# Input projection of a hybrid diffusion backbone: the order of its tiles, three convolution tiles between those of the queries

## Chip, cores and metric

The kernel runs on one core of one Trainium2 chip. Times are device microseconds of that core. TensorE (PE) multiplies matrices, PEld is its loading of weights, VectorE (DVE) and ScalarE (ACT) work elementwise, GpSimd (POOL) and SyncE (SP) issue DMAs, and POOL does a few small copies.

## What is computed

Two layers over 512 latent tokens (x) and 256 context tokens (ctx), model width 1024, float32. One input projection feeds three groups of heads; their outputs are joined and projected, and a SwiGLU feed-forward follows. The context takes part in the second layer only through its keys, values and GLA state.

```python
def layer(x, ctx, mod_x, mod_c, ..., ctx_out):
    hx = rmsnorm(x, g1) * (1 + sc1) + sh1
    hc = rmsnorm(ctx, g1) * (1 + csc1) + csh1
    (xc_in, xc_b, xc_c, xq, xk, xv, xgq, xgk, xgv, xgg, xlr) = jnp.split(hx @ w_in, COL_SPLITS, axis=-1)
    ...
    conv_x = short_conv(xc_in, xc_b, xc_c, conv_w)
    attn_x = window_attention(apply_rope(xq), apply_rope(xk), xv, k_ctx, v_ctx, sink)
    gla_x, gla_c = gla_bidir(xgq, xgk, xgv, xlr, xgg, ...)
    x = x + gt1 * (jnp.concatenate([conv_x, attn_x, gla_x], axis=-1) @ w_out)
    x = x + gt2 * swiglu(rmsnorm(x, g2) * (1 + sc2) + sh2, w_up, w_down)
    ...
```

## The kernel before, in words

Activations lie transposed, 128 features by up to 768 tokens. Every float32 operand of a dense product is split into a high and a low part, and a product is made of three: high by high, high by low, low by high. A **dense tile** (`dense_pass`, L754) makes 128 output columns: eight blocks of the contraction by three products, 24 matmuls of 512 columns for the latent tokens, and 24 of 256 for the context. Its weights come through a ring of four `raw` buffers; ScalarE casts the high part (`whi`) and VectorE subtracts for the low part (`wlo`, two buffers each), in `w_advance` (L541).

`IN_ORDER` (L427) lists the tiles of the input projection: `lr`, `gk`, `gq`, `gv`, `gg` of the GLA (its gates' input, keys, queries, values and output gate, two head pairs 0 and 1), `k`, `v`, `q0` to `q3` of the attention, and `cc`, `cx`, `cb` of the convolution (its two factors and its gate, two halves). The plan of weight loads (L463) and the loop that computes the tiles (L1888) both follow it. In the first layer one tile of modulation weights follows each of them, from the fifth on. In the second layer `q`, the convolution, `gq` and `gg` are made for the latent tokens alone.

Three things happen to a finished tile. `ev` (L1763) takes it out of its `main` bank of PSUM: a `q`, `v` or `cc` tile by a ScalarE copy, a `gk` tile by ScalarE and VectorE, `cx` by a VectorE product with `cc`, `cb` by five VectorE operations (three taps, product with the tile, split). `after` (L1836) prepares it: a `q` tile is rotated (four VectorE operations) and split (two more), `gq` starts a **GLA chain** (`gla_task`, L1284), and a `q` tile starts six attention blocks (four in the second layer; `attn_task`, L1481).

These chains are generators. A planner (`Plan`) keeps an estimated clock for each engine and, after each contraction block of a dense tile, lets those chains go a step whose inputs it thinks ready and whose buffers fit (`poll`, L294; `until`, L305). One GLA chain may be under way at a time, and three attention blocks. Behind the first tiles of a layer the exact order on each engine is no longer pinned (`S.strict = False`, L1901), and the framework's scheduler may still move single instructions.

A GLA chain forms gate values (matmuls with `gw`), then passes through seven levels. Each level is a group of 64x64 matmuls (a **gram**), a VectorE merge of its result (`COPY_PREDICATED`), two or three VectorE products on 128x768 elements that prepare the next level, and a ScalarE copy. An attention block is scores, maximum and sum on VectorE, exponentials on ScalarE, transposes, copies, value products, and a split into the tile `ca` that the second part of the output projection reads.

Behind the input projection stand the part of the output projection that reads convolution and GLA (`o1`, eight tiles), a wait for all attention blocks (L1922), and the part that reads attention (`o2`, L1952).

Temporary tiles come from a pool `t3` of 14 buffers, others from `act` of 20, PSUM from 3 `main` and 5 `bank` (L39). `cc`'s buffer is held until `cb` of the same half has been taken out.

Of the kernel before, what the change touches and what calls it, by code (L numbers as in the profile page):

```python
# [319 lines left out]
def hybrid_kernel(ctx: ExitStack, tc: tile.TileContext, x, c, cx, c_ctx, w_mod, b_mod, norm1_g, norm2_g,  # L320
# [97 lines left out]
    def out2_item(l, m, hold):  # L418
        def load(raw):
# [4 lines left out]
        w_item((l, "o2", m), 4, load, P, hold)  # L424

    N_OUT2, N_DOWN = 1, 3
    IN_ORDER = ("lr", "gk0", "gq0", "gv0", "k", "v", "q0", "gk1", "gq1", "gv1", "q1", "q2", "q3",  # L427
                "cc0", "cx0", "cb0", "cc1", "cx1", "cb1", "gg0", "gg1")
    IN_COL = dict(lr=W_LR, k=W_K, v=W_V)
    for i in range(2):  # L430
        IN_COL.update({f"gk{i}": W_GK + i * P, f"gq{i}": W_GQ + i * P, f"gv{i}": W_GV + i * P,
# [4 lines left out]
    def first_item(l, q):  # L436

        def load(raw):
            ks = slice(q * 2 * P, (q + 1) * 2 * P)
            r = []  # L440
            for i, name in enumerate(FIRST):
                for j in range(3 if name == "lr" else 1):
                    n, c0 = (32, IN_COL[name]) if name == "lr" else (P, IN_COL[name])
                    r.append((raw[:, :, i * P + j * n:i * P + (j + 1) * n],
                              w_in[l, ks, c0:c0 + n].rearrange("(k p) n -> p k n", p=P)))
            return r
        w_item((l, "first", q), 2, load, 4 * P)
        plan[-1]["quad"] = True
        plan[-1]["late"] = q > 0 or l == 0
        plan[-1]["apart"] = q + l == 0  # L450
# [9 lines left out]
    for l in range(DEPTH):  # L460
        for q in range(4 if l else 0):
            first_item(l, q)
        for i, name in enumerate(IN_ORDER):  # L463
            if name in FIRST:
# [1266 lines left out]
    for l in range(DEPTH):  # L1731
# [155 lines left out]
        X = None  # L1887
        for j, name in enumerate(IN_ORDER):  # L1888
            if name in FIRST:
# [194 lines left out]
```

## Time and profile before

| | |
|---|---|
| median of 3 runs | 1619.19 us (1618.64 to 1624.01) |
| the profiled execution | 1613.43 us, its span 1611.6 us |
| granted TensorE clock, mean | 0.997 |
| instructions | 29142 |
| DMA | 184.39 MB, 114 GB/s over the span |

The span runs from the first instruction to the last. In the first layer the tiles of the input projection behind the first four begin at 70 us and `o2` begins at about 391 us; in the second they begin at 988 us and `o2` at about 1216 us. A window's row gives the busy time of each engine in that stretch, and what is missing to its length is idle. An engine executes its own instructions in order, so an instruction that waits holds up those behind it.

### The profile page before, as it was taken

The page shows a single profiled execution, that of the slowest core. Times are in us where ns is not written, and L with a number is a line of the kernel's source. Part 1 is how long each engine was busy: PE and PEld are TensorE (multiplying, and loading weights), DVE is VectorE, ACT ScalarE, POOL GpSimd, SP SyncE. Part 2 cuts the span into 40 slices and gives each one's busy share as a digit, 9 for nine tenths or more (in the row PEclk, how much of TensorE's full clock was granted, in tenths as well). Part 3 has the DMA queues.
Part 4 walks back from the last instruction along what each step waited for, and adds up shares of the span by engine and source line. Part 5 has one row for each costly group of instructions (what it writes and reads, how often), then busy time and mean ns, then how long its engine had stood idle before and what let it go on. Part 6 is the DMA issues. An engine that isn't in the chain of part 4 may idle for free.

```text
span 1611.6 us, 29142 instructions
## 1 busy us (share of the span) xinstructions
PE 1569.9 (97%) x11530; PEld 1387.9 (86%) x11530; DVE 1219.3 (76%) x2426; ACT 757.0 (47%) x1596; POOL 105.2 (7%) x122
## 2 busy tenths in 40 slices
PE   7999999999999999999999999998999999999998
PEld 5778777888888899999999988786889989989898
DVE  5687886668886788788888877879787956747576
ACT  4455544453663243242433546464474744536354
POOL 2000000000000000000000010000001112213012
PEclk9999999999999999999999999999999999999999
DMA  9831222253224544435334342211225466858552
GB/s 256 247 113 28 82 64 71 62 170 109 75 79 146 156 132 144 143 118 156 93 108 127 91 133 66 53 40 41 66 85 120 94 148 139 173 126 160 147 123 93
DMA packets 277578, 184.39 MB, mean 114 GB/s; under 512 B 30853, under 2 KB 258753, under 8 KB 277441
## 3 DMA queue, kind: packets, MB, share of 16 engines
q1 hardware_dynamic: 251008, 155.93, 33.7%
q0 software_dynamic: 24608, 21.27, 7.7%
q10 hardware_dynamic: 1824, 5.31, 0.9%
q8 instruction: 91, 1.49, 0.4%
q14 instruction: 47, 0.38, 0.1%
HBM read 175.14 MB, written 7.34 MB: 113 GB/s over the span
## 4 chain that ended last, share of the span: by engine, by line
PE 75%; DVE 10%; DMA 3%; ACT 3%; issue 2%; DVEq 0%; SPq 0%; ACTq 0%
PE main L139 49%; PE bank L139 24%; DVE act L188 3%; PE bank L143 3%; DMA raw<-in_w_mod_dram 2%; DVE t L188 1%; DVE wlo L188 1%; DMA raw<-in_w_up_dram 1%; ACT t L155 1%; DVE t L216 1%; DVE t L199 1%; DVE mx L207 1%; ACT t L177 1%; DVE t L193 0%; ACT whi L177 0%
## 5 line engine op out<-in xcount | busy, mean ns | idle before, releaser
L139 PE MATMUL main<-act,whi 128*128 128x512 f32 (+2 forms) x2772 | 667.8, 345 | 5.6 <-DVE act L199 2.1
L139 PEld LDWEIGHTS main<-act,whi 128*128 128x128 f32 x2772 | 460.5, 189 | 63.6 <-issue 12.1
L139 PE MATMUL main<-act,wlo 128*128 128x512 f32 (+2 forms) x1866 | 477.7, 334 | 3.0 <-DVE wlo L188 3.0
L139 PEld LDWEIGHTS main<-act,wlo 128*128 128x128 f32 x1866 | 315.1, 189 | 31.7 <-DVE wlo L188 5.2
L177 ACT CAST whi<-raw 128x512 fp32r<-128x512 f32 (+4 forms) x242 | 181.5, 751 | 292.6 <-PE main L139 201.0
L139 PE MATMUL bank<-act,whi 128*128 128x256 f32 (+2 forms) x1140 | 208.9, 309 | 1.1 <-DVE whi L188 0.7
L139 PEld LDWEIGHTS bank<-act,whi 128*128 128x128 f32 x1140 | 178.5, 190 | 8.1 <-DVE whi L188 1.0
L139 PE MATMUL bank<-act,wlo 128*128 128x256 f32 (+2 forms) x898 | 171.7, 308 | 2.2 <-DVE wlo L188 2.2
L199 DVE SCALAR_TENSOR_TENSOR act<-main,mods,act 128x256 f32<-128x256 f32 (+1 forms) x162 | 99.1, 615 | 78.1 <-PE main L139 76.6
L139 PEld LDWEIGHTS bank<-act,wlo 128*128 128x128 f32 x898 | 142.8, 190 | 6.3 <-DVE wlo L188 3.2
L188 DVE TENSOR_TENSOR wlo<-raw,whi 128x1024 fp32r<-128x1024 f32 (+4 forms) x122 | 122.6, 1005 | 20.7 <-ACT whi L177 19.9
L188 DVE TENSOR_TENSOR wlo<-raw,wlo 128x512 fp32r<-128x512 f32 x120 | 81.6, 686 | 39.4 <-ACT wlo L177 38.7
L199 DVE SCALAR_TENSOR_TENSOR t<-raw,cst,t 128x512 f32<-128x512 f32 x126 | 92.1, 745 | 20.4 <-DMA raw<-in_w_mod_dram 19.8
L188 DVE TENSOR_TENSOR whi<-raw,whi 128x512 fp32r<-128x512 f32 x120 | 81.3, 686 | 26.2 <-ACT whi L177 24.6
L155 ACT ACTIVATE t<-bank,nm 128x256 f32<-128x256 f32 (+1 forms) x144 | 69.8, 497 | 60.4 <-DVE nm L199 55.7
L177 ACT CAST wlo<-raw 128x512 fp32r<-128x512 f32 x120 | 74.6, 622 | 40.9 <-PE main L139 17.4
L177 ACT COPY t<-bank 128x512 f32<-128x512 f32 (+3 forms) x131 | 57.4, 453 | 72.1 <-PE bank L139 43.5
L139 PE MATMUL main<-act 128*128 128x256 f32 (+1 forms) x516 | 79.5, 309 | 0.0
L188 DVE TENSOR_TENSOR act<-t,act 128x512 fp32r<-128x512 f32 (+7 forms) x110 | 73.1, 681 | 7.0 <-ACT act L177 5.2
L155 ACT ACTIVATE t<-t 128x256 f32<-128x256 f32 (+3 forms) x108 | 58.1, 538 | 41.8 <-DVE t L188 41.3
L139 PE MATMUL main<-t,whi 128*128 128x512 f32 (+1 forms) x302 | 75.9, 338 | 0.0
L139 PEld LDWEIGHTS main<-act 128*128 128x128 f32 x516 | 70.9, 191 | 5.2 <-ACT t L155 0.4
(162 smaller groups left out, 2007.3 us busy)
## 6 DMA issues: line engine op xcount, KB each, us to landing
raw<-in_w_mod_dram SPq DMA_DIRECT2D x92, 512.0 KB, 4.3
raw<-in_w_up_dram SPq DMA_DIRECT2D x80, 512.0 KB, 4.6
raw<-in_w_in_dram SPq DMA_DIRECT2D x26, 512.0 KB, 3.9
t<-in_w_up_dram POOLq DMA_DIRECT2D x40, 256.0 KB, 5.2
raw<-in_w_down_dram SPq DMA_DIRECT2D x24, 384.0 KB, 3.9
raw<-in_w_down_dram SPq DMA_DIRECT2D x32, 256.0 KB, 2.8
raw<-in_w_down_dram SPq DMA_DIRECT2D x16, 320.0 KB, 3.4
raw<-in_w_up_dram POOLq DMA_DIRECT2D x20, 256.0 KB, 4.7
```

The costliest lines, as they stand in the source:

```text
L139: self.pin("pe", self.nc.tensor.matmul(out, lhsT, rhs, start=start, stop=stop, **kw))
L143: self.pin("pe", self.nc.tensor.transpose(out, in_, ident))
L155: ins = self.pin("act", self.nc.scalar.activation(out, in_, func, **kw))
L177: self.pin("act", self.nc.scalar.copy(out, in_))
L188: self.pin(eng, self._v(eng).tensor_tensor(out, a, b, op))
L199: self.pin(eng, self._v(eng).scalar_tensor_tensor(out, a, s, b, op0, op1))
L207: self.pin("dve", self.nc.vector.tensor_reduce(out, in_, AX.X, op))
L216: self.pin("dve", self.nc.vector.copy_predicated(out, mask, data))
```

## The change

`IN_ORDER` is another list. `cc0` moves to the place behind `q0`, `cx0` to the place behind `q1`, `cb0` and `cc1` behind `q2`; `cx1`, `cb1` follow `q3`, and `gg0`, `gg1` stay last. Everything else is the same text, and the number of instructions of each kind on each engine is the same.

```diff
-    IN_ORDER = ("lr", "gk0", "gq0", "gv0", "k", "v", "q0", "gk1", "gq1", "gv1", "q1", "q2", "q3",
-                "cc0", "cx0", "cb0", "cc1", "cx1", "cb1", "gg0", "gg1")
+    IN_ORDER = ("lr", "gk0", "gq0", "gv0", "k", "v", "q0", "cc0", "gk1", "gq1", "gv1", "q1", "cx0", "q2", "cb0",
+                "cc1", "q3", "cx1", "cb1", "gg0", "gg1")
```

The first place is TensorE's order in the first layer, second GLA chain, ahead of its last gram (the last row of each piece; only its first matmul is shown). `main_2631` is the tile `cc0`, `t3_1816` and `t3_1817` the probabilities of an attention block that are being transposed. Before:

```order
L143 MATMUL bank_2538<-tab_82,t3_1816 128x128 x4
L143 MATMUL bank_2539<-tab_82,t3_1817 128x128 x4
L139 MATMUL main_2631<-act_496,wlo_2393 128x512
L139 MATMUL main_2631<-act_559,whi_2392 128x512 x2
L139 MATMUL main_2631<-act_559,wlo_2393 128x512
L139 MATMUL main_2631<-act_624,whi_2392 128x512 x2
L139 MATMUL main_2631<-act_624,wlo_2393 128x512
L139 MATMUL bank_2566<-act_2069,act_1317 64x64
```

Now, at the same place of the chain, where `main_2626` is the tile `cb0`:

```order
L143 MATMUL bank_2610<-tab_82,t3_2526 128x128 x2
L143 MATMUL bank_2610<-tab_82,t3_2527 128x128 x2
L139 MATMUL main_2626<-act_376,wlo_2414 128x512
L139 MATMUL main_2626<-act_431,whi_2413 128x512 x2
L139 MATMUL main_2626<-act_431,wlo_2414 128x512
L139 MATMUL main_2626<-act_496,whi_2413 128x512 x2
L139 MATMUL main_2626<-act_496,wlo_2414 128x512
L139 MATMUL main_2626<-act_559,whi_2413 128x512 x2
L139 MATMUL main_2626<-act_559,wlo_2414 128x512
L139 MATMUL main_2626<-act_624,whi_2413 128x512 x2
L139 MATMUL main_2626<-act_624,wlo_2414 128x512
L139 MATMUL bank_2643<-act_2122,act_1429 64x64
```

Between the last two grams stood 7 dense matmuls and 8 transposes; 18 dense matmuls and 4 transposes stand there now. The tile is `cb0` where it was `cc0`.

The second place is VectorE's order in the second layer, second GLA chain, around the merge of the fifth level. `act_11344`, `act_11345` and `act_10671` before, and `act_11360`, `act_11361` and `act_10780` now, are the chain's factors; `t3_11577` and `t3_11578` (now `t3_11593` and `t3_11594`) are probabilities of an attention block, `es` their scale. Before:

```order
L188 TENSOR_TENSOR act_10671<-act_10671,act_11345 128x24x2x16
L220 RECIPROCAL es_11583<-es_11583 128x2
L203 COPY t3_11508<-bank_11624 128x128
L193 TENSOR_SCALAR t3_11577<-t3_11577,es_11583 128x640
L193 TENSOR_SCALAR t3_11578<-t3_11578,es_11583 128x640
L216 COPY_PREDICATED t3_11348<-lvm_835,bank_11666 128x256
L216 COPY_PREDICATED t3_11348<-lvm_835,bank_11667 128x256
```

Now:

```order
L220 RECIPROCAL es_11599<-es_11599 128x2
L188 TENSOR_TENSOR act_10780<-act_10780,act_11361 128x24x2x16
L193 TENSOR_SCALAR t3_11593<-t3_11593,es_11599 128x640
L193 TENSOR_SCALAR t3_11594<-t3_11594,es_11599 128x640
L203 COPY t3_11524<-bank_11640 128x128
L199 SCALAR_TENSOR_TENSOR t3_11664<-t3_10670,vec_272,t3_11664 128x511
L216 COPY_PREDICATED t3_11364<-lvm_835,bank_11688 128x256
L199 SCALAR_TENSOR_TENSOR t3_11664<-t3_10670,vec_272,t3_11664 128x511
L216 COPY_PREDICATED t3_11364<-lvm_835,bank_11689 128x256
```

Two taps of `cb0` (L199, on 511 elements) now stand among the merges; they stood behind the chain's last level before.

The third place is TensorE's order in the first layer at the end of attention. The L143 rows are the last block's transposes, the 64x128 rows its value products. `main_4458` is the seventh tile of `o1`. Before:

```order
L139 MATMUL main_4458<-act_3582,wlo_4295 128x512
L143 MATMUL bank_4419<-tab_82,t3_4334 128x128 x4
L143 MATMUL bank_4420<-tab_82,t3_4335 128x128 x4
L139 MATMUL main_4458<-act_3697,whi_4294 128x512
L139 MATMUL bank_4421<-t3_4334,t3_1037 64x128
L139 MATMUL main_4458<-act_3697,whi_4294 128x512
L139 MATMUL main_4458<-act_3697,wlo_4295 128x512
L139 MATMUL main_4458<-act_3868,whi_4294 128x512 x2
L139 MATMUL bank_4421<-t3_4335,t3_1037 64x128
```

Now `main_4562` is the context half of the first tile of `o2`, whose last contraction block (`act_3797`) is attention's fourth group; for the context columns it is ready, for the latent ones it is what this last block makes:

```order
L139 MATMUL main_4562<-act_2766,wlo_4393 128x256
L139 MATMUL main_4562<-act_3797,whi_4392 128x256
L143 MATMUL bank_4480<-tab_82,t3_4438 128x128 x4
L143 MATMUL bank_4481<-tab_82,t3_4439 128x128 x4
L139 MATMUL main_4562<-act_3797,whi_4392 128x256
L139 MATMUL main_4562<-act_3797,wlo_4393 128x256
L139 MATMUL bank_4482<-t3_4438,t3_1037 64x128
L139 MATMUL bank_4529<-raw_4381,cst_144 32x256
L139 MATMUL bank_4482<-t3_4439,t3_1037 64x128
```

The last attention block stood within the seventh of eight `o1` tiles; now all of `o1` and most of the first `o2` tile stand ahead of it. Outside these stretches, that is, in the first chain's beginning, in the feed-forward and at the ends, each engine's order is the same as before but for single swaps of neighbours.

## Prediction

> **What bounds the kernel now.** I read the page first: busy time by engine, the slices, the chain that ended last.
>
> ```profile
> PE 1569.9 (97%) x11530; PEld 1387.9 (86%) x11530; DVE 1219.3 (76%) x2426; ACT 757.0 (47%) x1596; POOL 105.2 (7%) x122
> ...
> PEclk9999999999999999999999999999999999999999
> ...
> PE 75%; DVE 10%; DMA 3%; ACT 3%; issue 2%; DVEq 0%; SPq 0%; ACTq 0%
> ```
>
> TensorE is busy 97% of the span at its full clock and carries 75% of the chain. The change adds and removes no instruction, so it can win only what TensorE waits: 1611.6 - 1569.9 = 41.7 us. The windows show where (columns: window, length, then busy us of PE, PEld, DVE, ACT and POOL with counts, clock, DMA share, GB/s).
>
> ```profile
> 100.00:176.70 76.70, 73.85 (x819) 58.71 (x822) 63.84 (x145) 39.78 (x101) 2.35 (x2) 1.00 0.26 69
> 176.70:218.00 41.30, 36.64 (x556) 30.13 (x555) 39.44 (x71) 19.09 (x38) 2.29 (x2) 1.00 0.17 51
> 223.00:384.00 161.00, 160.72 (x1213) 131.75 (x1214) 109.39 (x293) 77.71 (x219) 2.19 (x4) 1.00 0.30 95
> 1070.60:1131.00 60.40, 54.22 (x528) 41.80 (x526) 56.35 (x115) 35.60 (x75) 1.55 (x2) 1.00 0.17 45
> 1085.00:1131.00 46.00, 39.81 (x463) 30.27 (x462) 44.70 (x97) 23.18 (x57) 1.55 (x2) 1.00 0.17 47
> 1131.00:1224.00 93.00, 92.75 (x639) 75.63 (x639) 71.03 (x178) 52.29 (x139) 2.93 (x4) 1.00 0.31 96
> ```
>
> Two stretches stand out, both the second GLA chain: **A** (layer 0, 176.7 to 218) with 41.30 - 36.64 = 4.7 us of idle TensorE, and **B** (layer 1, 1070.6 to 1131) with 60.40 - 54.22 = 6.2 us. VectorE is busy 39.44 of 41.30 us (95%) in A and 44.70 of 46.00 us (97%) in B's main part: there it sets the pace. Behind A and B TensorE idles 0.3 us in 161 and in 93 us, with VectorE at 68% and 76%. Who is waited for, in A and then in B (total us, times, longest):
>
> ```profile
> PE bank L139 <- DVE act L188: 2.1, 3, 0.8
> PE bank L139 <- ACT t L177: 1.8, 2, 1.4
> PE bank L139 <- DVE t L203: 0.5, 1, 0.5
> ...
> PE bank L139 <- ACT t L177: 1.8, 2, 1.4
> PE bank L143 <- DVE nm L199: 1.7, 1, 1.7
> PE main L139 <- DVE wlo L188: 1.7, 1, 1.7
> ```
>
> In B even a dense tile waits for its weights' low half, which stood late in VectorE's queue.
>
> **The change part by part.** TensorE's order, VectorE's and ScalarE's differ only from the first convolution tile to the first tile behind attention in each layer; all else stands as before. TensorE's prices, from steps of the timeline:
>
> ```profile
> 1079.15 0.62 PE L139 MATMUL main<-act,whi 128*128 128x512 f32 x2
> ...
> 1079.83 0.62 PE L139 MATMUL main<-act,whi 128*128 128x512 f32 x2
> ...
> 316.53 0.40 PE L139 MATMUL main<-act,whi 128*128 128x256 f32 x2
> ...
> 316.88 0.40 PE L139 MATMUL main<-act,whi 128*128 128x256 f32 x2
> ...
> 322.41 0.64 PE L139 MATMUL bank<-raw,cst 128*32 128x256 f32 x8
> ...
> 212.84 1.09 PE L143 MATMUL bank<-tab,t 128*128 128x128 f32 x8
> ...
> 319.49 1.31 PE L139 MATMUL bank<-t,t 128*64 128x128 f32 x20
> ```
>
> Three dense products of 512 columns take 0.68 us from step to step (0.227 each), three of 256 take 0.35 (0.12 each); four of the modulation 0.64 (two records each), eight transposes 1.09, ten value products 1.31 (two records each).
>
> *Stretch A.* From the chain's first gram to its last, the order counts 9 more dense products of 512, 12 more of 256, 12 more of the modulation, 8 transposes and 4 value products fewer: 2.04 + 1.44 + 1.92 - 1.09 - 0.52 = 3.8 us more work for TensorE. VectorE's list over the same levels changes by one rotation of a query tile fewer and the two products of cx0, one tap of cb0 and one weight split more: 0.1 us in all. If VectorE keeps the pace, A lasts 0.1 us longer and takes in 3.8 us that stood in the idle-free stretch behind it: **-3.7 us** (bounds: 0, and all idle of A, -4.7).
>
> *Stretch B.* From the gate products to the last gram: 11 more dense products of 512, 12 of 256, 6 transposes: 2.50 + 1.44 + 0.82 = 4.8 us. VectorE's list grows here (prices from B, the last two rows from behind it: count, busy us, mean ns, idle before):
>
> ```profile
> L188 DVE TENSOR_TENSOR wlo<-raw,whi 128x1024 fp32r<-128x1024 f32 x6 | 7.3, 1218 | 0.0
> L188 DVE TENSOR_TENSOR act<-t,act 64x512 fp32r<-64x512 f32 x6 | 4.1, 686 | 0.2
> L203 DVE COPY t<-bank 128x512 f32<-128x512 f32 x3 | 2.0, 683 | 0.0
> L199 DVE SCALAR_TENSOR_TENSOR t<-bank,t 128x512 f32<-128x512 f32 x1 | 0.7, 692 | 8.2 <-ACT t L155 8.2
> L188 DVE TENSOR_TENSOR t<-main,t 128x512 f32<-128x512 f32 x1 | 0.7, 682 | 0.0
> ...
> L199 DVE SCALAR_TENSOR_TENSOR t<-t,vec,t 128x511 f32<-128x511 f32 x2 | 1.5, 742 | 0.0
> ...
> L188 DVE TENSOR_TENSOR act<-t,act 128x512 fp32r<-128x512 f32 x1 | 0.7, 694 | 0.0
> ```
>
> One weight split (1.22), cb0's two taps (1.48), product (0.68) and split (0.69) and one copy (0.68) come in, two splits of a query tile (1.37) and one statistics step (0.69) go: +2.7 us; smaller ones cancel within 0.2. B therefore grows by 2.7 and takes in 4.8: **-2.1 us** (bounds: 0 and -6.2).
>
> *First chain, layer 0.* gk1's two copies on VectorE leave it, since the tile moves behind cc0; TensorE idles 76.70 - 73.85 = 2.9 us around there. The larger takes some 0.7, as the copies of 512 below. I take 0 (bounds 0 and -0.7), since that chain's waits are short and spread.
>
> *The end of attention, layer 0.* q3 comes four tiles later, and its last block's transposes now stand behind the first output tile's products instead of a tile and a half before them. Before:
>
> ```profile
> 370.13 0.23 PE L139 MATMUL bank<-trib,identb 128*128 128x128 bf16 x1
> ...
> 380.62 1.04 PE L143 MATMUL bank<-tab,t 128*128 128x128 f32 x8
> ...
> 381.30 0.59 ACT L177 COPY t<-bank 128x512 f32<-128x512 f32 x1 [2.51 <-PE bank L143]
> ...
> 381.94 0.68 DVE L203 COPY t<-bank 128x512 f32<-128x512 f32 x1
> ...
> 383.42 1.09 PE L139 MATMUL bank<-t,t 128*64 128x128 f32 x14
> ```
>
> The transposes end at 381.7, the copies at 382.6, the rest of the value products start at 383.4, with dense products between. In the new order two products of 256 and one of the modulation stand there: 0.24 + 0.16 = 0.4 us of cover for a wait of 0.9 to 1.8. **+1.0 us** (bounds 0 and 1.4). The high and low halves behind it are covered by seven modulation products (1.1 us). Queued behind this wait is the whole output projection; nothing else is late. In layer 1 the last block belongs to the second half of the columns, and seven tiles of the first half stand ready: 0.
>
> *DMAs.* The weights' loads move on SP's queue in the same order as the tiles; their number and sizes stay, and the rows of A and B show the DMA engines 17% busy: 0.
>
> [...] The idle gaps of A and B repeat by level of the chain. [...] The rows of waits name results still being made in a VectorE that is 95% busy, so the trace speaks for the engine; no run here shows the buffers' part.
>
> Sum: -3.7 - 2.1 + 0 + 1.0 = **-4.8 us**. The profiled execution took 1613.43 us (span 1611.6 and 1.8 around it), so 1608.6 for it; the median of the runs shown, 1619.19, lies 5.8 above that execution, so I forecast **1614.4**.
>
> **The rivals.**
>
> *The chain's latency, not VectorE's load, sets A and B.* A gram waits for its factors by way of ScalarE (1.8 us of the waits in each). Dense products put between the grams then push the grams back, and each stretch grows by what it takes in: A and B give 0, the end costs 1.0: **1620.2**. For it: half the waits end elsewhere than on a VectorE that is late. Against: VectorE is never idle for long.
>
> *All waits go.* If the smoother mix leaves VectorE's queue short wherever TensorE looks, A gives 4.7 and B 6.2 and the end is covered: -10.9, **1608.3**.
>
> *Attention becomes the tail (slower).* The buffer held longer, and q3's late start, put one attention block off by one pass of its chain. From scores to transposes that took 380.6 - 370.1 = 10.5 us before; the new order puts 27 products of 512 (6.1), 34 of 256 (4.1) and ten value products (1.3) between them, 11.5 us, a reserve of 1.0. A block late by a chain leaves TensorE standing 9.5 us ahead of the output projection, with nothing to run: 1614.4 + 9.5 = **1623.9**. It decides once attention is more than 1.0 + 4.8 us late. [...] Against it: TensorE's new order has all but the last block's work done ahead of that point.
>
> **How the numbers follow.** Forecast 0.50, latency 0.22, all waits go 0.16, tail 0.12. About 0.3% (4.9 us) is what a measurement of this kernel can tell from no change. The forecast's own bounds (1611 to 1618) lie on both sides of it: faster 0.30, same 0.20. With the others: faster 0.46, same 0.20 + 0.22 + 0.04 = 0.46, slower 0.08. The range leaves out the worst tails only: 1608 to 1621.5.
>
> **What would show it.** Right: in layer 0's second chain TensorE idle about 1 us instead of 4.7 with VectorE still over 90%; in B about 4 us; one wait of about a microsecond for a copy ahead of the output projection's last products. Wrong: VectorE well below 90% in A with TensorE still waiting (latency); a wait of several microseconds on attention in front of the output projection (tail); new gaps in 223 to 384.

## The result, and the profile after

The changed kernel takes 1626.01 us (median of 12 runs, 1623.86 to 1637.75), the kernel before 1619.10 (12 runs on the same chip, 1615.99 to 1624.01): a ratio of 1.0051, 95% interval 1.0035 to 1.0067. It is slower by half a per cent, where a gain of 4.8 us was forecast. The profiled execution of the changed kernel took 1632.61 us, span 1630.8, so it lies 6.6 above its median, as that of before lies 5.7 below its own. Of the 19.2 us between the two spans, then, a good part belongs to these two executions and not to the change.

The page of the changed kernel, its busy time, its clock and the chain that ended last:

```profile
PE 1579.9 (97%) x11523; PEld 1395.0 (86%) x11530; DVE 1219.3 (75%) x2426; ACT 755.8 (46%) x1596; POOL 107.2 (7%) x122
...
PE   7999999989999999999999999999989999999998
...
PEclk9999999999999999999999999999999999999999
...
PE 71%; DVE 11%; DMA 5%; ACT 3%; issue 2%; DVEq 0%; ACTq 0%; SPq 0%
```

TensorE has the same work and is busy for 10.0 us longer (1579.9 against 1569.9), and its idle time is 1630.8 - 1579.9 = 50.9 us, 9.2 more than before. So the 19.2 us have two halves: waits, and matmuls that ran slower. TensorE's share of the chain falls from 75% to 71%, that of DMAs rises from 3% to 5%. In the slices, each of 41 us, the clock shows nothing, and the waits show as a single 8 in TensorE's row, in the slice from 326 to 367 us, where before has a 9. The windows show more. The first two are the second chain of layer 0 from its first gram to its last, before and then changed; the others are of the changed kernel: the stretch behind that, the start of the output projection and what follows it, the second chain of layer 1, and the start of layer 1's output projection (columns as in the prediction; the clock is third from the end):

```profile
176.50:217.30 40.80, 36.48 (x557) 30.14 (x556) 38.94 (x70) 19.29 (x38) 1.81 (x2) 1.00 0.18 52
```

```profile
182.60:225.80 43.20, 40.54 (x585) 32.45 (x585) 36.76 (x67) 16.25 (x33) 2.03 (x2) 1.00 0.28 75
...
228.00:334.00 106.00, 105.76 (x800) 85.93 (x800) 71.45 (x186) 51.60 (x137) 2.15 (x4) 1.00 0.28 89
334.00:350.00 16.00, 11.18 (x60) 9.19 (x53) 7.65 (x23) 7.11 (x18) 0.00 (x0) 0.79 0.31 108
350.00:389.00 39.00, 39.00 (x306) 31.82 (x307) 28.91 (x77) 15.19 (x50) 0.00 (x0) 1.00 0.27 84
1087.00:1145.50 58.50, 55.39 (x528) 42.91 (x527) 55.74 (x113) 31.91 (x67) 2.16 (x2) 0.97 0.21 57
1178.00:1198.00 20.00, 15.77 (x84) 12.10 (x81) 14.28 (x35) 14.46 (x32) 0.00 (x0) 0.91 0.14 35
```

Idle TensorE falls in A from 40.80 - 36.48 = 4.3 (4.7 in the prediction, whose window ends 0.7 us later) to 43.20 - 40.54 = 2.7 us and in B from 6.2 to 58.50 - 55.39 = 3.1. Two new holes stand where before had none: 4.8 us between 334 and 350, where layer 0's output projection begins, and 4.2 us between 1178 and 1198, the same place of layer 1. Who is waited for there, first in layer 0, then in layer 1 (total us, times, longest):

```profile
PE bank L143 <- DVE t L193: 4.8, 1, 4.8
...
PE bank L143 <- DVE t L193: 3.0, 2, 1.7
PE main L139 <- ACT t L155: 1.0, 1, 1.0
PE main L139 <- ACT act L177: 0.3, 1, 0.3
```

L193 is the scaling of an attention block's probabilities, which TensorE wants to transpose. In layer 0 VectorE's load is not the cause, as the timeline of ScalarE and VectorE in the changed kernel shows (start, length, and in brackets the idle time ahead of it with what ended it):

```profile
330.12 0.87 ACT L177 COPY t<-bank 128x512 f32<-128x512 f32 x2 [0.26 <-PE bank L143]
...
332.03 0.16 DVE L199 SCALAR_TENSOR_TENSOR nm<-mx,nsink 128x2 f32<-128x2 f32 x1
...
337.18 1.04 ACT L177 CAST whi<-raw 128x1024 fp32r<-128x1024 f32 x1 [6.19 <-DMA raw<-in_w_out_dram]
338.13 0.47 ACT L155 ACTIVATE t<-bank,nm 128x256 f32<-128x256 f32 x1
```

ScalarE stands for 6.19 us in front of the cast of an output projection tile's weights, whose load has not landed. The attention's exponentials (L155), which need only the maximum `nm` of 332.03, stand behind that cast. The load is late for the reason that the DMA issues show. First the changed kernel between 324 and 342 us, then before in the same window (engine, count, KB each, median us from issue to landing):

```profile
act<-away POOLq DMA_DIRECT2D x3, 768.0 KB, 6.5
...
raw<-in_w_out_dram SPq DMA_DIRECT2D x2, 256.0 KB, 9.0
```

```profile
act<-away POOLq DMA_DIRECT2D x4, 768.0 KB, 7.2
...
raw<-in_w_out_dram SPq DMA_DIRECT2D x2, 256.0 KB, 4.0
```

`act<-away` is `fetch`: the residual stream, put out to DRAM for the time of the input projection, is brought back in four tiles of 768 KB by POOL's queue once `act` buffers are free. Before, the weights' load left at 324.5 and the fetch began at 329.0. In the new order three of the four tiles leave from 326.7 on (the first had left at 295.2); the load leaves at 327.6, beside them, and lands after 9.0 us in place of 4.0. How the DMA engines share their time between the two queues is not in these rows.

The other half is the clock. Windows right behind the waits, and then two of before, around the first of them:

```profile
339.90:346.70 6.80, 5.94 (x22) 5.38 (x23) 3.33 (x13) 4.15 (x11) 0.00 (x0) 0.50 0.45 157
...
1192.00:1198.00 6.00, 4.70 (x22) 4.35 (x23) 3.89 (x10) 4.92 (x8) 0.00 (x0) 0.72 0.02 4
```

```profile
334.00:350.00 16.00, 16.00 (x127) 12.45 (x125) 10.01 (x23) 7.74 (x19) 0.00 (x0) 1.00 0.54 198
...
339.90:346.70 6.80, 6.80 (x57) 5.85 (x56) 3.57 (x8) 0.92 (x3) 0.00 (x0) 1.00 0.41 138
```

For 6.8 us behind layer 0's wait TensorE gets half its clock (0.50) and shows 22 matmuls where before shows 57 (the sizes differ in part). The changed kernel has five such stretches between 30 and 1600 us, at 340, 534, 1128, 1193 and 1394 us, and the profiled execution of before has none there. Windows of 2 us put what they lose at 10.2 us of full clock, close to the 10.0 us by which TensorE is busy longer. Two of the five, with 3.4 of these 10.2 us, lie in the feed-forwards (534 and 1394 us), where the order is as before. The idle time is divided in the same way: in the long stretches behind the attention of each layer (395 to 1000 us and 1240 to the end; before, 390 to 985 and 1224 to the end) TensorE idles 18.5 us where before idles 14.9. So of the 19.2 us some 7 lie where the change moved nothing.

### The profile page after: what moved, and what is told of

Its sections match the earlier page's. It is cut to its first block, busy times and chain, and to the rows that moved or that the text cites. A ratio compares the mean times of both kernels' runs of the same rounds, so it can differ in the third digit from the quotient of the medians.

```text
span 1630.8 us, 29141 instructions
## 1 busy us (share of the span) xinstructions
PE 1579.9 (97%) x11523; PEld 1395.0 (86%) x11530; DVE 1219.3 (75%) x2426; ACT 755.8 (46%) x1596; POOL 107.2 (7%) x122
## 4 chain that ended last, share of the span: by engine, by line
PE 71%; DVE 11%; DMA 5%; ACT 3%; issue 2%; DVEq 0%; ACTq 0%; SPq 0%
PE main L139 45%; PE bank L139 23%; DMA raw<-in_w_mod_dram 3%; DVE act L188 3%; PE bank L143 3%; DVE wlo L188 2%; DMA raw<-in_w_up_dram 2%; ACT t L155 1%; DVE t L188 1%; DVE t L199 1%; DVE mx L207 1%; DVE t L216 1%; ACT whi L177 1%; DVE act L199 1%; DMA raw<-in_w_out_dram 1%
## 5 line engine op out<-in xcount | busy, mean ns | idle before, releaser
L199 DVE SCALAR_TENSOR_TENSOR act<-main,mods,act 128x256 f32<-128x256 f32 (+1 forms) x162 | 99.0, 615 | 82.2 <-PE main L139 81.0
L199 DVE SCALAR_TENSOR_TENSOR t<-raw,cst,t 128x512 f32<-128x512 f32 x126 | 92.2, 746 | 19.0 <-DMA raw<-in_w_mod_dram 18.2
L155 ACT ACTIVATE t<-bank,nm 128x256 f32<-128x256 f32 (+1 forms) x144 | 69.8, 497 | 61.8 <-DVE nm L199 53.3
L155 ACT ACTIVATE t<-t 128x256 f32<-128x256 f32 (+3 forms) x108 | 58.1, 538 | 41.6 <-DVE t L188 41.0
```

Source lines behind the costliest of these rows:

```text
L155: ins = self.pin("act", self.nc.scalar.activation(out, in_, func, **kw))
L199: self.pin(eng, self._v(eng).scalar_tensor_tensor(out, a, s, b, op0, op1))
```

## The experiments

All were compared with the kernel before on the same chip. "us" is the median of the kernel's runs; the ratio is to before, with its 95% interval; the clock is the mean over the kernel's runs (before: 0.9950 over 111 runs; 0.9964 over the seven beside e13 to e15).

| run | us | ratio to before | clock |
|---|---|---|---|
| the change | 1626.0 | 1.0051 (1.0035 to 1.0067) | 0.9928 |
| e1_layer0_only | 1627.2 | 1.0058 (1.0036 to 1.0081) | 0.9933 |
| e2_layer1_only | 1623.7 | 1.0027 (1.0010 to 1.0044) | 0.9933 |
| e3_fetch_behind | 1624.0 | 1.0028 (1.0012 to 1.0044) | 0.9936 |
| e4_cast_on_use | 1627.4 | 1.0048 (1.0022 to 1.0074) | 0.9932 |
| e5_cc0_only | 1619.8 | 1.0016 (0.9999 to 1.0032) | 0.9937 |
| e6_one_scratch_less | 1619.9 | 1.0021 (1.0007 to 1.0036) | 0.9928 |
| e7_before_fetch_behind | 1616.9 | 1.0004 (0.9988 to 1.0020) | 0.9958 |
| e8_conv_between_late | 1622.0 | 1.0032 (1.0021 to 1.0043) | 0.9941 |
| e9_q3_late_only | 1620.6 | 0.9989 (0.9972 to 1.0005) | 0.9943 |
| e10_layer0_fetch_behind | 1621.0 | 1.0005 (0.9989 to 1.0021) | 0.9948 |
| e11_wait_5us | 1631.7 | 1.0060 (1.0041 to 1.0079) | 0.9920 |
| e12_wait_2us | 1623.9 | 1.0024 (1.0007 to 1.0042) | 0.9947 |
| e13_after_6_banks | 1644.4 | 1.0149 (1.0132 to 1.0166) | 0.9915 |
| e14_before_6_banks | 1638.4 | 1.0128 (1.0113 to 1.0143) | 0.9900 |
| e15_after_6_banks_fetch | 1649.2 | 1.0195 (1.0180 to 1.0210) | 0.9900 |
| e16_gates_no_silu | 1628.2 | 1.0045 (1.0028 to 1.0061) | 0.9932 |
| e17_before_gates_no_silu | 1621.5 | 0.9996 (0.9984 to 1.0008) | 0.9949 |

### Which layer

e1 and e2 give each layer an order of its own.

```diff
-    for i, name in enumerate(IN_ORDER):
+    for i, name in enumerate(IN_ORDERS[l]):
```

> The new order in layer 0 alone, the old one in layer 1. Queue theory (in layer 0 the load of the second weight tile of the output projection lands late beside the x tiles that are fetched back, its cast on ScalarE stands ahead of the attention's exps, and TensorE waits): the wait of about 5 us at the start of layer 0's output projection is there, and most of the loss with it: 4 to 7 us above before. Rival 'both layers' (each layer loses about alike, by the attention that starts later): 2 to 4 us above before.

> The new order in layer 1 alone, the old one in layer 0. Queue theory: layer 1's wait at the same place is smaller (the waits between 1182 and 1193 us of the profile after, 4.4 us together), so 0 to 3 us above before, and layer 0 as before. Rival 'both layers': 2 to 4 us above before.

Layer 0 alone costs 5.8 thousandths (9.4 us), more than was expected, layer 1 alone 2.7 (4.4 us), also more. Added up they pass the whole change by 3.4 thousandths, about what the three intervals leave open, so the sizes of the shares are uncertain, not their signs. In layer 1 the windows show gain and loss side by side, first of e2, then of before:

```profile
1070.00:1130.00 60.00, 56.90 (x497) 43.92 (x495) 54.28 (x108) 34.82 (x71) 2.18 (x2) 0.97 0.20 54
1165.00:1190.00 25.00, 20.77 (x144) 16.15 (x142) 17.47 (x45) 17.56 (x41) 0.00 (x0) 0.93 0.16 36
```

```profile
1070.00:1130.00 60.00, 53.81 (x524) 41.55 (x524) 55.35 (x114) 35.60 (x75) 1.55 (x2) 1.00 0.17 45
1165.00:1190.00 25.00, 24.95 (x167) 20.20 (x168) 19.46 (x53) 19.59 (x48) 2.16 (x3) 1.00 0.28 85
```

In the second chain TensorE waits 56.90 - 53.81 = 3.1 us less, at the end of attention 24.95 - 20.77 = 4.2 us more, and both windows run at a lower clock than before.

### Layer 0: the load behind the fetch

```diff
-            nc.gpsimd.dma_start(xs[j][:, :, :n], away[j][:, :, :n])
+            S.pin("sp", nc.sync.dma_start(xs[j][:, :, :n], away[j][:, :, :n]))
```

> The new order in both layers; the x tiles are fetched back by SP's queue in place of POOL's, so that they stand behind the weights' load. Queue theory: the load of the second weight tile of layer 0's output projection lands within 5 us of its issue instead of 9, its cast starts 3 to 4 us earlier, the wait of 4.8 us for the attention falls below 1.5 us, and the time comes back to 1616 to 1621 us. Rival 'attention late' (TensorE has run out of other work because the queries' last tile comes four tiles later, whatever the loads do): the wait stays above 3 us and the time at 1624 to 1628. A third way: the x tiles now land later and the first residual additions wait for them; then a wait by DMA shows there and the time is above 1624.

> As e1_layer0_only (new order in layer 0, old in layer 1), with the x tiles fetched back by SP's queue. Queue theory: all that layer 0 loses is the wait behind the fetch and the lower clock after it, so 1616 to 1620 us, at most 2 us above before, against 1627 for e1_layer0_only, with no wait over 1 us between 330 and 350 us. Rival (layer 0's order costs by itself): 1622 or more.

> The kernel before, with the x tiles fetched back by SP's queue as in e3_fetch_behind: the control to it. Queue theory: before has no wait there that the fetch could cause (the second load of the output projection lands 4 us after its issue), so 2 us below to 2 us above before. Rival (the fetch on SP's queue is better in any order, and says nothing on the change): 2 us or more below before.

On SP's queue the fetch starts behind the load: in e3 the load leaves at 328.5 us, the fetch at 329.4. TensorE's order stays what it was in the changed kernel. The DMA issues of e3 between 324 and 342 us:

```profile
act<-away SPq DMA_DIRECT2D x4, 768.0 KB, 8.7
...
raw<-in_w_out_dram SPq DMA_DIRECT2D x2, 256.0 KB, 3.1
```

And its windows, at layer 0's output projection and at layer 1's:

```profile
335.00:351.00 16.00, 16.00 (x124) 12.96 (x117) 10.95 (x40) 9.26 (x31) 0.00 (x0) 1.00 0.61 234
...
1169.00:1189.00 20.00, 15.77 (x82) 12.07 (x80) 14.25 (x35) 14.46 (x32) 0.00 (x0) 0.91 0.36 119
```

The load lands after 3.1 us, the wait of 4.8 us is gone and the half clock behind it too (clock 1.00, 124 matmuls in 16 us against 60); layer 1 keeps its hole to a hundredth. The time was expected at 1616 to 1621 and came to 1624.0; what is left above before, 2.8 thousandths, is what layer 1 alone costs in e2 (2.7), which the expectation counted as small. e10, with layer 0 alone, closes this: 1.0005 against e1's 1.0058, from nothing but the queue of the fetch (four DMAs in each layer; every other instruction keeps its place on its engine). The same window in e1 and then in e10:

```profile
334.00:350.00 16.00, 11.78 (x71) 9.27 (x68) 8.01 (x25) 7.42 (x19) 0.00 (x0) 0.89 0.39 136
```

```profile
334.00:350.00 16.00, 16.00 (x124) 12.90 (x117) 10.98 (x40) 9.45 (x31) 0.00 (x0) 1.00 0.60 229
```

The control e7 doesn't move: in the old order the load is early enough (in before it leaves at 324.5 us, the fetch at 329.0), so the other queue is no gain by itself.

```diff
         w_item((l, "o1", j), 4, load, 256)
+        plan[-1]["late"] = j == 1
```

> The new order in both layers; the second weight tile of the output projection is cast when it is used, not one tile ahead, so its cast stands behind the attention's exps on ScalarE. The loads are as in the changed kernel. Queue theory: the wait of 4.8 us for the attention falls below 1.5 us; TensorE may wait 1 to 2 us for the cast instead; 1619 to 1623 us. Rival 'attention late': the wait stays above 3 us, 1625 to 1629 us.

e4 was a miss of design. Its edit moves the cast in the program's text alone: once built, each engine has its instructions in the same order as in the changed kernel. The cast still stands ahead of the exponentials on ScalarE, which is idle for 6.8 us in front of it, and TensorE waits 5.5 us in the same place. So e4 says nothing on the cast; it is the changed kernel run once more (1.0048, against 1.0051).

### Layer 1: the end of attention

e5 and e9 take the order apart.

```diff
 e5
-    ... "q0", "cc0", "gk1", "gq1", "gv1", "q1", "cx0", "q2", "cb0", "cc1", "q3", "cx1", "cb1", ...
+    ... "q0", "cc0", "gk1", "gq1", "gv1", "q1", "q2", "q3", "cx0", "cb0", "cc1", "cx1", "cb1", ...
 e9
+    ... "q0", "gk1", "gq1", "gv1", "q1", "q2", "cc0", "cx0", "cb0", "cc1", "q3", "cx1", "cb1", ...
```

> Of the three moved tiles only cc0 stays early (behind q0); q2 and q3 follow q1 as before, and cx0 stands behind q3. Theory now: layer 1's waits before the output projection (1.1, 1.4 and 1.9 us) come from cc0, whose product holds a scratch tile from then on, so that the planner starts attention later: 190 of TensorE's instructions of the attention are left behind the first output tile in layer 1 (194 in the changed kernel, 128 before), and the three waits stay (3 to 5 us together); layer 0 has as many left as before (158) and loses its wait of 4.8 us. So 0 to 4 us above before. Rival 'q3 late': the waits of layer 1 are gone (below 1 us together), and the time is 2 us below to 1 us above before.

> Only q3 moves: behind cc0, cx0, cb0 and cc1, which all stand behind q2; nothing of the convolution stands between q0 and q2. With e5_cc0_only it divides layer 1's late attention between its two candidates. 'q3 late matters': waits for the attention of 1 us or more together ahead of layer 1's output projection, though cc0 is not early; 1 to 4 us above before. 'cc0 early alone matters': no wait over 0.5 us there, within 1 us of before. In layer 0 the fetch stands on POOL's queue: if the load of the second tile of the output projection is issued beside it again, the wait of some 5 us is there in this order too, and the time 4 us or more above before.

Waits of TensorE between 1165 and 1200 us, in e5 and then in e9; before has none there over 0.3 us:

```profile
PE bank L143 <- DVE t L193: 2.4, 1, 2.4
```

```profile
PE bank L139 <- DVE t L203: 1.8, 1, 1.8
PE bank L143 <- DVE t L193: 0.8, 1, 0.8
```

Either move alone makes a hole (2.4 and 2.6 us), the changed kernel with both the larger one (4.2); so neither theory had it alone. Neither kernel is shown slower than before (e5's interval begins at 0.9999, e9's ends at 1.0005), so no run here shows what a hole of this smaller size costs. Layer 0's wait is in neither, and in e9 the load of the output projection left at 320.4, ahead of three of the fetch's four tiles, and landed after 3.9 us.

Three things could pace that end: a scratch tile, the PSUM banks, ScalarE's order. Each was tried.

```diff
 e6
-ROOM = dict(main=3, bank=5, act=20, t3=14)
+ROOM = dict(main=3, bank=5, act=20, t3=13)
 e13, e14, e15
+ROOM = dict(main=2, bank=6, act=20, t3=14)
 e16, e17
-                S.act(g, src, AF.Silu)
+                S.acopy(g, src)
```

e16 and e17 leave out the Silu of the output gates, so that ScalarE has no function table to load for it (1.28 us a load in e3); e16 has e3's edit as well.

> The kernel before, with 13 scratch tiles in place of 14, and nothing else. If a held scratch tile is what makes layer 1's attention late, waits for the attention's probabilities of 2 us or more together turn up ahead of layer 1's output projection, where before shows none over 0.3 us, and the time is 1 to 6 us above before. Rival (the order itself, not the tile, makes the attention late): no such waits, and within 2 us of before.

e6 has no wait at the end of attention in layer 1, so one scratch tile fewer does not make the hole. It is slower all the same, by 2.1 thousandths, at a mean clock of 0.9928 against 0.9958 of before on that chip. Its profiled execution, the fastest of its runs, shows only a part of this, in layer 1's second chain (TensorE idle 7.0 us where before idles 6.2, and a clock of 0.89):

```profile
1070.00:1130.00 60.00, 52.99 (x463) 41.95 (x463) 54.45 (x111) 32.33 (x68) 0.52 (x1) 0.89 0.19 54
```

> The changed kernel with 6 shared PSUM banks and 2 for the dense products, in place of 5 and 3. A task of the attention needs 3 shared banks, so of 5 only one task runs at a time, and its tail is a chain that the tiles of the convolution, once moved ahead of it, no longer cover. Bank theory: all of the attention stands ahead of the output projection in both layers (none of it behind the first output tile, against 175 and 194 instructions of TensorE), the waits for it there (4.8 us in layer 0, 4.4 in layer 1) are gone, and the time comes to 1612 to 1621 us. Rival (the tail is bound by ScalarE's and VectorE's own time, not by banks): waits of 3 us or more for the attention turn up ahead of the output projection instead, and the time is 1624 or more. Rival 2: two banks for the dense products make TensorE wait for evictions, many small waits all over, 1630 or more.

> The kernel before with the same 6 and 2 banks. Bank theory: before hides its attention behind the output projection, so there is less to gain: 4 us below to 1 us above before. Rival 2 as above: 1625 or more.

> e13_after_6_banks with the x tiles fetched back by SP's queue: within 2 us of e13_after_6_banks if no attention is left that the load of the output projection's weights could hold up; 3 us or more below it if that load still makes a wait.

The bank theory fell. With six banks the program of e13 has no attention left behind the first output tile, and TensorE waits ahead of it all the same. The waits of e13 between 1190 and 1220 us, and behind them one over its whole span; then those of e14 between 1200 and 1230:

```profile
PE bank L143 <- DVE t L193: 4.0, 1, 4.0
...
PE main L139 <- DVE act L199: 8.2, 11, 1.6
```

```profile
PE bank L143 <- DVE t L193: 3.5, 2, 2.2
```

The wait for evictions (L199) was 2.0 us in the changed kernel and is 8.2 in e13: two banks are fewer than the dense products want, and all three kernels are 1.3 to 2.0% slower than before, the old order too. e15 met neither of its ranges: it came out 4.8 us above e13, where at most 2 us above or 3 us below had been expected, and its 4.0 us wait at this place is the same; where the 4.8 us come from stays open. e14, in the old order, also waits 3.5 us for the probabilities, once 36 of the attention's instructions are left behind layer 1's first output tile in place of 128. This fits an end of attention that is no shorter in the old order but has products of the output projection among it; since e14 also has one bank fewer for the dense products, it does not prove it.

> e3_fetch_behind (both layers in the new order, the x tiles fetched back by SP's queue) without the Silu of the gates gg0 and gg1: the gates are copied as they are, so the output differs, and ScalarE doesn't change its function table there and back (two loads of 1.28 us to each gate pass, ahead of the attention's exps). Theory 'ScalarE's order paces the tail': layer 1's waits for the attention (1.1, 1.4, 1.9 us in e3_fetch_behind) fall to 1.5 us together or less, and the time lies 0 to 3 us above its own control e17. Rival 'the chain's own length paces it': the waits stay at 3 us or more together, and it lies 3 to 6 us above e17, as e3_fetch_behind does above before.

> The control: the kernel before, with the gates copied in the same way (the Silu left out). Before has no waits for the attention ahead of the output projection, so only what the table loads cost elsewhere can go: 4 us below to 1 us above before.

In e3 four table loads of 1.28 us stand on ScalarE at this place, in e16 none. The same 35 us of e3 and then of e16, and behind them who is waited for in e16, between 1165 and 1200 and then between 1215 and 1230 us:

```profile
1165.00:1200.00 35.00, 30.77 (x198) 23.99 (x197) 24.22 (x62) 21.49 (x52) 0.00 (x0) 0.95 0.23 76
```

```profile
1165.00:1200.00 35.00, 32.80 (x211) 25.17 (x212) 24.22 (x58) 16.76 (x46) 0.00 (x0) 1.00 0.25 83
```

```profile
PE bank L143 <- DVE t L193: 1.3, 1, 1.3
PE main L139 <- ACT t L177: 0.7, 1, 0.7
...
PE bank L143 <- DVE t L193: 1.9, 1, 1.9
```

Without the table loads the hole falls from 4.2 to 2.2 us, and a new wait of 1.9 us for the probabilities stands later, at 1220 us. In time nothing is won: e16 lies 4.9 thousandths (7.9 us) above e17, more than either theory had. The planner also orders TensorE's attention anew once the loads are gone, so this is no clean test: the table loads may hold up to half of the hole, and they are not all of it. For the rest the length of the last tasks' own chain (scores, maximum, exponentials, scale, transposes), with too few dense products beside it, is what no run has ruled out. No run here makes this chain alone longer or shorter, so that much stays open.

### The price of a wait

A chain of copies on GpSimd, with a transposition on TensorE that waits for its end, stands ahead of `o2` in layer 0 of the kernel before.

```diff
         S.kept = {}
+        if l == 0:
+            xw, p0 = tmp(), bank()
...
+            for i in range(6):                      # e12: 2
+                S.pin("pool", nc.gpsimd.tensor_copy(xw[:, b_], xw[:, a_]))
+            S.pin("pe", nc.tensor.transpose(p0[:, P:2 * P], xw[:, 0:128], ident))
```

> The kernel before, with a chain of copies on GpSimd put in ahead of layer 0's second half of the output projection, and a transposition on TensorE that waits for its end: an idle TensorE of 4 to 6 us at a place where nothing waited. 'A wait costs its length': 4 to 6 us above before, mean granted clock as before. 'A wait of this length costs the clock as well': a stretch of 3 to 7 us at half clock right behind it, and 1.7 to 3.4 us more, 6 to 9 us above before.

> The same with fewer copies: an idle TensorE of 2 to 3 us at the same place. 'Length': 2 to 3 us above before. 'Clock as well': a half-clock stretch behind it in some executions only, since the kernel before has waits of 2 us without one: 2 to 4 us above before, the mean clock between that of before and that of e11_wait_5us.

The wait and the stretch behind it, in e11 and then in e12:

```profile
PE bank L1934 <- POOL t L1933: 4.9, 1, 4.9
```

```profile
393.00:400.00 7.00, 3.57 (x9) 2.90 (x10) 2.84 (x4) 2.47 (x4) 3.06 (x6) 0.52 0.68 187
```

```profile
PE bank L1934 <- POOL t L1933: 2.3, 1, 2.3
```

```profile
395.00:400.00 5.00, 4.83 (x16) 3.92 (x17) 1.51 (x3) 1.85 (x3) 0.11 (x1) 0.66 0.70 188
```

A wait of 4.9 us costs 6.0 thousandths, 9.7 us (6.6 to 12.8), and the mean clock falls from 0.9947, that of before on the same chip, to 0.9920. One of 2.3 us costs 3.9 us (1.1 to 6.8); its profiled execution shows a short half-clock stretch, but the mean clock of its runs (0.9947) is that of before. So a wait of the size of layer 0's cost about twice its length here. For the short one the interval holds its length as well as twice its length; the unchanged mean clock speaks for its length in most executions.

### A version that beats both

e8 was meant as one.

```diff
+    ... "q0", "gk1", "gq1", "gv1", "q1", "cc0", "q2", "cx0", "q3", "cb0", "cc1", "cx1", "cb1", ...   # layer 0 alone, with e3's edit
```

> A try at a version that beats both: layer 1 in the old order; layer 0 with q1, cc0, q2, cx0, q3, cb0, so that the attention's instructions that are left behind the first output tile fall to 8 from 158; the x tiles fetched back by SP's queue. Theory: no wait for the attention is left at layer 0's output projection, the second chain keeps its idle time of before, so 3 us below to 1 us above before. Rival (attention that is taken in earlier is missing as filling later): 2 to 6 us above.

Behind layer 0's second chain, in e8 and then in before:

```profile
223.00:330.00 107.00, 103.26 (x794) 83.60 (x793) 73.61 (x215) 52.19 (x168) 0.00 (x0) 0.98 0.19 55
```

```profile
223.00:330.00 107.00, 106.76 (x795) 87.58 (x795) 70.09 (x191) 53.28 (x149) 0.61 (x1) 1.00 0.24 73
```

Its rival held: no wait at the output projection, but TensorE idles 3.7 us in this stretch, where before idles 0.2. e7 and e9 are no slower than before, and not shown faster. No run beats the kernel before.

## Why the prediction was wrong

*Stretch A, -3.7.* Mis-sized, and the step that failed in it is "if VectorE keeps the pace, A lasts 0.1 us longer". From the first gram to the last TensorE took in 40.54 - 36.48 = 4.1 us more work, near the forecast 3.8; but the stretch grew by 43.20 - 40.80 = 2.4 us, though VectorE's work in it fell from 38.94 to 36.76 us. VectorE was forecast above 90% busy and is at 85%, with TensorE still waiting: the sign that was named for the first rival, the chain's latency, which had A grow by all that it takes in. A gave 4.32 - 2.66 = 1.7 us; with the wait for a copy right behind the last gram, 1.0 us before and 1.7 now, it gave 1.0.

*Stretch B, -2.1.* Right in kind: 6.2 to 3.1 us, where about 4 was forecast, with VectorE at 55.74 of 58.50 us (95%). e2 shows the same fall of 3.1 us.

*The end of attention in layer 0, +1.0.* No such wait; the window from 350 to 389 us is full to its hundredths. The wait stands at the other end, at the start of the output projection.

*The end of attention in layer 1, 0.* This step failed. It looked only at the last block's place and counted the tiles that stood ready beside it, not the blocks ahead of it; the dense tiles that were moved forward were the cover of the end of attention. That the new order makes the hole is shown by e2, e5 and e9; that it does so by taking away the cover is argued, and ScalarE's table loads may hold a part of it. TensorE idles 4.2 us there, more than B gains. The rival "attention becomes the tail" came nearest to this mechanism, with the chance of 0.12 and at one place of layer 0 instead, and two of its signs came: a wait of several microseconds on attention in front of the output projection, and new gaps between 223 and 384 us. Its cause in layer 0 was another, though, the late load, so that its 1623.9 us lies near the measured 1626.0 is luck.

*DMAs, 0.* This step failed too, and is the larger one in layer 0. It reasoned from the average share in A and B (17%) and from the order within SP's queue, and did not look at POOL's queue at the place where both carry transfers; the window of before at 334 to 350 us, shown above, has the DMA engines 54% busy. The order of the loads stayed; their time against the fetch did not. That is 4.8 us of wait, and in time, with the clock, 3.7 us (the change against e3, 1.0051 against 1.0028, whose intervals overlap a little) to 8.6 us (e1 against e10, whose intervals don't).

*The clock, not a term at all.* The sum counted idle time at its length. Over 263 runs of fifteen kernels here (before, the changed one, e1 to e12, e17), with a level for each kernel and one slope, a mean clock that is lower by 0.001 goes with 1.65 us more. By this line, which is a correlation, the changed kernel stands 4.5 us above before at equal clock, and its lower clock (0.9928 against 0.9950) goes with 3.6 us more. The traces show where the clock falls: behind the 4.8 us of layer 0 it is 0.50 for 6.8 us, behind the waits of 1.0 to 1.7 us in layer 1 it is 0.72 over the 6 us from 1192, behind the 2.3 us of e12 0.66 over 5 us. What decides whether it falls behind a wait, no run here shows.

*The buffers' part*, which the prediction left open, does not show for the scratch tile that `cc0` holds: e6 takes one away and gets no wait at the end of attention. In the chains themselves it moves the idle time both ways: 4.4 us in place of 5.3 between 176 and 223 us, 7.0 in place of 6.2 between 1070 and 1130.

## What to carry to other kernels

In a kernel whose bottleneck engine is 97% busy, as here, filling one hole takes the filling from another place (in e2 TensorE idles 3.1 us less in the second chain and 4.2 us more at the end of attention): look there for a chain that now stands uncovered, and count from its first task, not its last. When instructions move, compare the moment of each transfer with those of the other queues and look at what stands behind its consumer on the same engine (here exponentials, behind a cast that waited 6.19 us for its load); an average DMA share, 17% here, did not show that. And where, as here, the clock falls behind a wait, price a new wait of TensorE of several microseconds at about twice its length (4.9 us cost 9.7 in e11, 6.6 to 12.8).

## What the hardware showed that was not expected

Half-clock stretches follow waits well below the 4.8 us of layer 0. In layer 1 of the changed kernel there are two waits for the probabilities (3.0 us together, the longest 1.7) and one of 1.0 ahead of them, within 12 us, and the clock is 0.72 in the 6 us from 1192 (0.50 from 1194 to 1196). A single short wait can do the same, and need not: in layer 0's feed-forward TensorE waits once for an eviction, 1.6 us in the changed kernel and 1.9 us at the same place of before, and only the shorter wait is followed by half clock (0.50 from 535 to 537 us). First the changed kernel, then before:

```profile
532.00:538.00 6.00, 5.06 (x14) 3.79 (x15) 4.69 (x9) 0.00 (x0) 0.00 (x0) 0.72 0.64 173
```

```profile
522.00:528.00 6.00, 4.15 (x20) 3.07 (x19) 5.93 (x10) 0.73 (x2) 0.00 (x0) 1.00 0.63 185
```

So at this size the length of the wait alone does not decide. The other surprise is the load: two transfers of 256 KB took 9.0 us beside a fetch from another queue that was issued 0.8 us earlier, and 3.1 us with the fetch behind them on their own queue, with the same data and sizes.
